# AdaLN half rows of a hybrid decoder layer: loads 0.6 of a spacing ahead, multiplies kept in program order, the loaded rows finished at a switch of buffers

## The chip, the cores and the metric

The kernel runs on one core of a Trainium2 chip. The metric is the device time of one execution in microseconds (us); lower is better. A profiled execution gives the trace from which the rows below are taken.

## The reference, cut to what matters

One decoder layer: a mixer of eight attention heads beside an RG-LRU recurrence, then an MLP. Each of the two halves of the layer is modulated by six vectors (shift, scale and gate for the mixer, the same for the MLP), which come from one product of the conditioning vector with a wide matrix.

```python
c_act = silu(c)                                     # [1, 2048]
mod = (c_act @ w_ada[l] + b_ada[l]).reshape(B, 6, 2048)
sh1, sc1, gt1, sh2, sc2, gt2 = mod

h = rmsnorm(x, g_norm_mix[l]) * (1.0 + sc1) + sh1
q, k, v, xr, xg = split(h @ w_in[l])                # 5 x 1024 columns, 512 tokens
o_attn = stick_breaking_attention(q, k, v)          # 8 heads of 128
xr = causal_depthwise_conv(xr, w_conv, b_conv)
o_lru = rg_lru(xr, ...) * gelu(xg)
mixed = concat(rmsnorm(o_attn), rmsnorm(o_lru))
x = x + gt1 * (mixed @ w_out[l])

h = rmsnorm(x, g_norm_mlp[l]) * (1.0 + sc2) + sh2
x = x + gt2 * (square(relu(h @ w_mlp_in[l])) @ w_mlp_out[l])
```

All of it is float32: 2048 model columns, 512 tokens, 8192 hidden columns.

## The kernel before

**Products.** TensorE (PE) does a float32 product as three products of fp32r operands: high weight by high operand, high weight by low operand, low weight by high operand (`mm3`, lines 259, 262 and 263; for v lines 467 to 469). `weights()` makes the two parts: SP, the engine that issues the loads, loads a raw block `wr`; ScalarE (ACT) copies it to `wh` (line 244, the high part); VectorE (DVE) subtracts that from `wr` to `wl` (line 122). There are four `wr` buffers and three each of `wh` and `wl`, and the three instructions are hoisted by a priority of 150. A step of a product is one such block: 12 matmuls over four PSUM banks. The banks are emptied by ACT (line 459, high part) and DVE (line 460, low part) for queries and keys.

**Attention and recurrence.** While the projections run, three lanes of background work (`bg`, `bgl`, `bg2`) are advanced by `tick()`, once for each step of a product. Each lane is a queue of generators that yield how many steps to wait. `bg` holds the pairs of attention heads: scores, their soft terms (ACT lines 637 to 639 and 644, DVE lines 635 and 641), `shares` (PE line 654) and values. `bgl` holds the recurrence: the convolution (DVE line 556), the gates (ACT line 566 and DVE line 122 split the input into an `x` tile, then PE; line 572 and 575 the sigmoids), and the scans (ACT lines 583, 587, 588 and 592, DVE lines 589, 595 and 597).

**AdaLN rows.** `bg2` holds `adas(m)` for the first gate GT1 and for the scale and shift of the MLP, SC2 and SH2. One of the 16 rows of such a vector is 128 of its columns, on 128 partitions: two half rows of the matrix, each 128 x 1024 (512 KB), loaded by SP (line 199), multiplied on DVE by the broadcast `silu(c)` in `cb` with a sum along the row (line 211), and joined by a small instruction (line 220). `pace` is the spacing of the rows in steps: 3.2 in the v product, 1.6 in the first eight steps of the product for heads 4 and 5, then 3.2 again.

**Buffers of the rows.** In the first part the half rows use the four `x` tiles alone (`MID`). These tiles hold also the split inputs of the gates and two tiles of each scan. Behind the product for the first half of the gate branch (`xg_group(0)`) the rows switch to `LATE`, which takes `x` and `tt` tiles in turn, with five half rows loaded ahead.

**Order.** A scheduler places the instructions of an engine by priority and by when their inputs are to be had, unless `later()` pins one: it then stays behind the instruction that was traced last before it on its engine. Loads of half rows are always pinned on SP. Their multiplies are pinned only in `LATE`, where each half is asked for by its number (`q` given). On the chip each engine does its instructions in the order so fixed.

Of the kernel before, what the change touches and what calls it, by code (L numbers as in the profile page):

```python
# [64 lines left out]
def hybrid_layer_kernel(  # L65
# [32 lines left out]
    def T(tag, dt=F32, cols=None):  # L98
        return new(next(split_tag) if tag == "w4" else tag, dt, cols)
# [48 lines left out]
    def col(base, j):  # L148
        return vec[:, base + j : base + j + 1]
# [29 lines left out]
    def later(ins):  # L179
        return tc.keep_in_program_order(ins)  # L180


    def mod(m, j):
        return mods[:, m * NK + j : m * NK + j + 1]

    class Rows:
# [15 lines left out]
        def row(self, m, j, tags, q=None):  # L202

            i = m * NK + j
            if q in (None, 0):
                self.ga = T("ga")
            for q_ in (0, 1) if q is None else (q,):
                if (i, q_) not in self.tiles:
                    self.load(2, tags)
                t = self.tiles.pop((i, q_))  # L210
                ins = stt(
                    out=t, in0=t, scalar=1.0, in1=cb[q_], op0=ALU.mult, op1=ALU.mult, accum_out=self.ga[:, q_ : q_ + 1],
                )
                if q is not None:
                    later(ins)
                del t
                if tags is not MID:
                    self.load(1, tags)
            if q != 0:
                stt(  # L220
                    out=mod(m, j), in0=self.ga[:, 0:1], scalar=self.ga[:, 1:2], in1=col(C_BADA, i), op0=ALU.add, op1=ALU.add,
                )

    rows, rows2 = Rows(SC1, SH1), Rows(GT1, SC2, SH2)
    MID = itertools.cycle(["x"])
# [73 lines left out]
    bg, bgl, bg2 = Lane(), Lane(), Lane()  # L299
# [300 lines left out]
    def lru_out(o0):  # L600
        for o in range(o0, o0 + 4):
            act(xg_t[o], xg_t[o], AF.Gelu_apprx_tanh)
        yield 1.0
        for o in range(o0, o0 + 4):
            g = xg_t[o]
            tt(out=g, in0=conv_y[o], in1=g, op=ALU.mult)
            add_square(acc_l, g, T("n"), o == 0)
            yield 1.0
# [89 lines left out]
    def adas(m):  # L698
        for j in range(NK):
            if tags2[0] is MID:  # L700
                rows2.row(m, j, MID)
                yield pace[0]
            else:
                for q in range(2):
                    rows2.row(m, j, LATE, q)
                    yield pace[0] / 2
        ready.add(m)

    pace = [3.2]
# [26 lines left out]
    def xg_group(o0, tags):  # L736
        bs = [bank(t) for t in tags]

        def evac(b):
            t = T("a")  # L740
            copy(b, t, bs[b])
            xg_t[o0 + b] = t

        group(bs, range(NK), lambda k: w_in[blk(k), XG + o0 * P : XG + (o0 + 4) * P], lambda k: hT[k], evac)
# [4 lines left out]
    bg.drain()  # L749
    bg.add(pair(2))  # L750
    bg2.add(adas(GT1), adas(SC2), adas(SH2))
    v_group(4)
    bg.drain()
# [14 lines left out]
    bg.add(attn_mix())  # L768
    bgl.add(lru_out(0))
    tags2[0] = LATE  # L770
    rows2.load(5, LATE)
    xg_group(4, BANKS[4:])
    bg.drain()
# [588 lines left out]
    tags = ["w4"] * 3 + ["w3"] * 2 + ["w4"] * 2 + ["w3"]  # L1362
# [108 lines left out]
```

## Time and profile before

| What | Value |
|---|---|
| Three timed runs | 1986.9, 1987.16, 1989.67 us; median 1987.16 |
| Profiled execution | 1982.96 us, of which the span is 1981.3 |
| Mean granted clock of TensorE | 0.996 |
| DVE line 211 from 237 to 530 us | 50 multiplies, 60.7 us, 1218 ns each |
| ACT table loads from 337 to 452 us | 13, 16.7 us |

A row of the timeline has the start and the duration in us, the engine, the line of the source, the operation, output and inputs, the shape of the tiles, and in brackets for how long the engine had been idle and what released it. A row of the groups has the count, then the busy time in us and the mean in ns, then the idle time ahead of it. A row of the waits has the engine, what it was about to write and its line, whom it waited for, the sum in us, how many times, and the longest. SPq is SP's own queue of instructions that issue loads; a row of the issues has the count, KB each, and the median time from issue to landing.

### The profile page before, as it was taken

To read this page: it belongs to the slowest core of one execution; us is meant where nothing else is said; L and a number is where in the kernel's file an instruction comes from. 1 tells how busy PE (TensorE), PEld (TensorE's weight loads), DVE (VectorE), ACT (ScalarE), POOL (GpSimd) and SP (SyncE) were. 2 spreads that over 40 slices of the span, in tenths; PEclk is the share of its full clock that TensorE was granted. 3 is DMA by queue.
4 is the path that set the end of the run, shared out by engine and by line. 5 is a ranking of instruction groups with operands and counts; after the bars stand their busy time and mean duration, and the time that the engine had idled before them with its cause. 6 is when DMAs were issued, how large, how long until landed. Compare 5 with 4: busy or idle time off the path is not lost.

```text
span 1981.3 us, 37180 instructions
## 1 busy us (share of the span) xinstructions
PE 1936.3 (98%) x14148; PEld 1813.5 (92%) x14148; DVE 1760.7 (89%) x2979; ACT 1077.1 (54%) x1580; POOL 193.4 (10%) x307
## 2 busy tenths in 40 slices
PE   8999999999999998999999999999999999999997
PEld 6778888788888998999999999999999999999996
DVE  8998786888998599999999999999989779879986
ACT  4443564786433386565555556556445545555542
POOL 0000000000000000112112211200000210211100
PEclk9999999999999999999999999999999999999998
DMA  9896655556779543756656665755677667669653
GB/s 365 306 331 214 205 172 186 183 157 217 226 244 373 176 139 114 239 187 223 211 182 196 223 194 184 235 186 195 234 260 284 247 249 269 232 248 343 215 198 112
DMA packets 205238, 443.51 MB, mean 224 GB/s; under 512 B 20481, under 2 KB 42113, under 8 KB 205058
## 3 DMA queue, kind: packets, MB, share of 16 engines
q1 hardware_dynamic: 176338, 356.58, 54.4%
q0 software_dynamic: 23680, 77.61, 10.6%
q10 hardware_dynamic: 5040, 6.93, 1.1%
q8 instruction: 111, 1.82, 0.4%
q14 instruction: 69, 0.57, 0.1%
HBM read 376.30 MB, written 64.75 MB: 223 GB/s over the span
## 4 chain that ended last, share of the span: by engine, by line
PE 53%; DVE 3%; DMA 1%; issue 1%; ACT 1%; POOL 0%; DVEq 0%; POOLq 0%; ACTq 0%; SPq 0%
PE ps_mm L1104 9%; PE ps_mm L1102 9%; PE ps_mm L1103 9%; PE ps_z L1103 7%; PE ps_z L1104 7%; PE ps_z L1102 7%; PE ps_o L1104 2%; PE ps_o L1102 2%; PE ps_o L1103 2%; DVE w L122 1%; DVE ts L1060 0%; DMA a<-sum 0%; DMA a<-part 0%; DVE a L1357 0%; DVE a L122 0%
## 5 line engine op out<-in xcount | busy, mean ns | idle before, releaser
L1102 PE MATMUL ps_mm<-a,w 128*128 128x256 f32 x1696 | 467.7, 276 | 1.5 <-ACT w L1072 0.5
L1103 PE MATMUL ps_mm<-a,w 128*128 128x256 f32 x1696 | 468.2, 276 | 0.3 <-DVE a L122 0.3
L1104 PE MATMUL ps_mm<-a,w 128*128 128x256 f32 x1696 | 468.1, 277 | 0.3 <-DVE w L122 0.3
L1104 PE MATMUL ps_z<-a,w 128*128 128x256 f32 x1304 | 361.1, 277 | 6.9 <-DVE w L122 6.7
L1103 PE MATMUL ps_z<-a,w 128*128 128x256 f32 x1304 | 360.7, 277 | 0.2
L1102 PE MATMUL ps_z<-a,w 128*128 128x256 f32 x1304 | 360.7, 277 | 0.1
L1072 ACT ACTIVATE w<-ts 128x1024 fp32r<-128x1024 f32 x244 | 258.2, 1058 | 169.6 <-DVE ts L1068 158.0
L1066 ACT ACTIVATE w<-raw 128x768 fp32r<-128x768 f32 x244 | 205.1, 841 | 259.5 <-PE ps_mm L1103 81.7
L122 DVE TENSOR_TENSOR w<-ts,w 128x1024 fp32r<-128x1024 f32 x244 | 297.7, 1220 | 52.9 <-PE ps_mm L1103 16.7
L1102 PEld LDWEIGHTS ps_mm<-a,w 128*128 128x128 f32 x1696 | 318.2, 188 | 2.1 <-ACT w L1072 0.7
L1104 PEld LDWEIGHTS ps_mm<-a,w 128*128 128x128 f32 x1696 | 318.4, 188 | 0.8 <-DVE w L122 0.7
L1103 PEld LDWEIGHTS ps_mm<-a,w 128*128 128x128 f32 x1696 | 318.5, 188 | 0.5 <-DVE a L122 0.5
L122 DVE TENSOR_TENSOR w<-raw,w 128x768 fp32r<-128x768 f32 (+1 forms) x296 | 267.2, 904 | 41.1 <-ACT w L244 24.9
L1104 PEld LDWEIGHTS ps_z<-a,w 128*128 128x128 f32 x1304 | 245.2, 188 | 8.2 <-DVE w L122 8.1
L1103 PEld LDWEIGHTS ps_z<-a,w 128*128 128x128 f32 x1304 | 245.3, 188 | 0.8 <-DVE a L122 0.8
L1102 PEld LDWEIGHTS ps_z<-a,w 128*128 128x128 f32 x1304 | 245.3, 188 | 0.5 <-ACT ps_z L1090 0.3
L244 ACT ACTIVATE wh<-wr 128x512 fp32r<-128x512 f32 (+1 forms) x184 | 113.2, 618 | 144.3 <-PE ps_mm L262 61.8
L259 PE MATMUL ps_mm<-a,wh 128*128 128x512 f32 x448 | 176.1, 393 | 2.4 <-ACT wh L244 1.2
L263 PE MATMUL ps_mm<-a,wl 128*128 128x512 f32 x448 | 174.8, 391 | 0.9 <-DVE wl L122 0.7
L262 PE MATMUL ps_mm<-a,wh 128*128 128x512 f32 x448 | 174.6, 390 | 0.0
L1060 DVE TENSOR_TENSOR ts<-raw 128x512 f32<-128x512 f32 x244 | 166.5, 683 | 6.4 <-DMA raw<-in_w_mlp_out_dram 5.6
L122 DVE TENSOR_TENSOR wl<-wr,wh 128x512 fp32r<-128x512 f32 (+1 forms) x184 | 123.5, 673 | 30.5 <-ACT wh L244 30.2
(334 smaller groups left out, 4011.2 us busy)
## 6 DMA issues: line engine op xcount, KB each, us to landing
raw<-in_w_mlp_out_dram SPq DMA_DIRECT2D x124, 512.0 KB, 4.6
raw<-in_w_mlp_in_dram SPq DMA_DIRECT2D x120, 512.0 KB, 3.8
x<-in_w_adaT_dram SPq DMA_DIRECT2D x108, 512.0 KB, 5.4
wr<-in_w_in_dram SPq DMA_DIRECT2D x160, 256.0 KB, 3.3
tt<-in_w_adaT_dram SPq DMA_DIRECT2D x52, 512.0 KB, 6.4
part<-a POOLq DMA_DIRECT2D x84, 256.0 KB, 4.2
a<-part SPq DMA_DIRECT2D x84, 256.0 KB, 6.2
n<-in_w_adaT_dram SPq DMA_DIRECT2D x64, 256.0 KB, 4.2
```

What stands on the lines that cost most here:

```text
L122: tt(out=out, in0=full, in1=f32(high), op=ALU.subtract)
L244: act(h[:, :n], r[:, :n], AF.Copy)
L259: first = mm(out, wh, ah, start=start, stop=False, **kw)
L262: mm(out, wh, al, start=False, stop=False, **kw)
L263: mm(out, wl, ah, start=False, stop=stop, **kw)
L1060: tt(out=t[:, : 2 * HT].rearrange("p (a b) -> p a b", a=2), in0=r[:, HT : 3 * HT].rearrange("p (a b) -> p a b", a=2), in1=r[:, q_(0)].unsq ...
L1066: act(h, r[:, HT:], AF.Copy)
L1072: act(h, t, AF.Copy)
L1102: mm(out, wh[:, blk(i)], ah, start=st, stop=False, **kw)
L1103: mm(out, wh[:, blk(i)], al, start=False, stop=False, **kw)
L1104: mm(out, wl[:, blk(i)], ah, start=False, stop=j == js[-1], **kw)
```

## The change

```diff
@@ class Rows, row()
                 ins = stt(
                     out=t, in0=t, scalar=1.0, in1=cb[q_], op0=ALU.mult, op1=ALU.mult, accum_out=self.ga[:, q_ : q_ + 1],
                 )
-                if q is not None:
+                if q is not None or tags is MID:
                     later(ins)
@@ def adas(m)
             if tags2[0] is MID:
+                rows2.load(2, MID)
+                yield 0.6 * pace[0]
                 rows2.row(m, j, MID)
-                yield pace[0]
+                yield 0.4 * pace[0]
@@ behind xg_group(0)
     tags2[0] = LATE
+    while rows2.tiles:
+        bg2.next()
     rows2.load(5, LATE)
     xg_group(4, BANKS[4:])
```

In `MID` a row's two loads are issued 0.6 of the spacing before its multiplies; the multiplies are pinned behind the DVE instruction traced last; and at the switch to `LATE` the rows that have been loaded are multiplied before the five loads ahead are issued. The number of loads, multiplies and matmuls is the same. The lines of the changed kernel stand two or four further down behind the added ones. The order of all engines moves with it from the v product on to the second half of the gate branch, in three places as follows. In the rows a name is a tile with its running number, `x` a half row or a tile of the recurrence, `ga` the two sums of a row, `wr`, `wh` and `wl` a block of weights and its parts, `ps_` a PSUM bank, `a` and `n` work tiles, `vec` and `spl` constants.

DVE near the end of the v product, where the last v banks are emptied (line 484) and the product for heads 4 and 5 begins, before:

```order
L484 TENSOR_TENSOR a_2857<-ps_mm_2389,a_2856 128x256
L211 SCALAR_TENSOR_TENSOR x_3000,ga_2999<-x_3000,cb_81 128x1024
L484 TENSOR_TENSOR a_2861<-ps_mm_2389,a_2860 128x256
L484 TENSOR_TENSOR a_2857<-ps_mm_2390,a_2856 128x256
L211 SCALAR_TENSOR_TENSOR x_3002,ga_2999<-x_3002,cb_82 128x1024
L484 TENSOR_TENSOR a_2861<-ps_mm_2390,a_2860 128x256
L220 SCALAR_TENSOR_TENSOR mods<-ga_2999,vec 128x1
L362 TENSOR_TENSOR n_1849<-n_1849,tt_2768 128x512
L484 TENSOR_TENSOR a_2898<-ps_mm_2391,a_2897 128x256
L211 SCALAR_TENSOR_TENSOR x_3026,ga_3025<-x_3026,cb_81 128x1024
L122 TENSOR_TENSOR wl_2948<-wr_2945,wh_2947 128x512
```

DVE at the same place in the changed kernel:

```order
L484 TENSOR_TENSOR a_2853<-ps_mm_2389,a_2852 128x256
L484 TENSOR_TENSOR a_2857<-ps_mm_2389,a_2856 128x256
L484 TENSOR_TENSOR a_2853<-ps_mm_2390,a_2852 128x256
L484 TENSOR_TENSOR a_2857<-ps_mm_2390,a_2856 128x256
L362 TENSOR_TENSOR n_1849<-n_1849,tt_2764 128x512
L484 TENSOR_TENSOR a_2898<-ps_mm_2391,a_2897 128x256
L211 SCALAR_TENSOR_TENSOR x_2812,ga_2887<-x_2812,cb_81 128x1024
L122 TENSOR_TENSOR wl_2944<-wr_2941,wh_2943 128x512
```

Of three multiplies ahead of the block of weights one is left.

DVE between the masks of the first scores of heads 4 and 5 and the first line 641 of that head, which the shares wait for through ACT, before:

```order
L597 SCALAR_TENSOR_TENSOR a_2386<-a_1028,a_2386 128x512
L122 TENSOR_TENSOR wl_3526<-wr_3523,wh_3525 128x512
L595 TENSOR_TENSOR a_2473<-x_3282,a_2473 128x512
L595 TENSOR_TENSOR a_2516<-x_3282,a_2516 128x512
L597 SCALAR_TENSOR_TENSOR a_2473<-a_1030,a_2473 128x512
L597 SCALAR_TENSOR_TENSOR a_2516<-a_1032,a_2516 128x512
L556 SCALAR_TENSOR_TENSOR a_3511<-a_1034,vec,a_3511 128x511
L211 SCALAR_TENSOR_TENSOR x_3516,ga_3515<-x_3516,cb_81 128x1024
L122 TENSOR_TENSOR wl_3575<-wr_3572,wh_3574 128x512
L122 TENSOR_TENSOR wl_3629<-wr_3626,wh_3628 128x512
L556 SCALAR_TENSOR_TENSOR a_3511<-a_1034,vec,a_3511 128x510
L641 SCALAR_TENSOR_TENSOR tt_3433<-ps_z_3418,tt_3433 128x512
```

DVE at the same place in the changed kernel:

```order
L597 SCALAR_TENSOR_TENSOR a_2386<-a_1028,a_2386 128x512
L595 TENSOR_TENSOR a_2469<-x_3282,a_2469 128x512
L122 TENSOR_TENSOR wl_3571<-wr_3568,wh_3570 128x512
L597 SCALAR_TENSOR_TENSOR a_2469<-a_1030,a_2469 128x512
L595 TENSOR_TENSOR a_2516<-x_3282,a_2516 128x512
L211 SCALAR_TENSOR_TENSOR x_3388,ga_3468<-x_3388,cb_81 128x1024
L211 SCALAR_TENSOR_TENSOR x_3390,ga_3468<-x_3390,cb_82 128x1024
L122 TENSOR_TENSOR wl_3629<-wr_3626,wh_3628 128x512
L641 SCALAR_TENSOR_TENSOR tt_3429<-ps_z_3414,tt_3429 128x512
```

A scan (line 597) and two steps of the convolution (line 556) have moved behind line 641, and the two multiplies of a row stand side by side ahead of it.

ACT in the first recurrence, where its functions change between the sigmoids of the gates (lines 572 and 575) and the functions of the scans (lines 583 and 587), before:

```order
L575 ACTIVATE ps_z_3135<-ps_z_3135,vec 128x512
L583 ACTIVATE x_3281<-a_1026,spl 128x512
L1422 ACT_TABLE_LOAD
L244 ACTIVATE wh_3210<-wr_3208 128x256
L587 ACTIVATE a_1026<-a_1026,nspl 128x512
L1422 ACT_TABLE_LOAD
L244 ACTIVATE wh_3227<-wr_3225 128x512
L572 ACTIVATE a_1028<-ps_z_3168,vec 128x512
```

ACT at the same place in the changed kernel:

```order
L575 ACTIVATE ps_z_3215<-ps_z_3215,vec 128x512
L583 ACTIVATE x_3281<-a_1026,spl 128x512
L244 ACTIVATE wh_3297<-wr_3295 128x512
L583 ACTIVATE x_3281<-a_1028,spl 128x512
L244 ACTIVATE wh_3323<-wr_3321 128x512
L572 ACTIVATE a_1032<-ps_z_3248,vec 128x512
L575 ACTIVATE ps_z_3253<-ps_z_3253,vec 128x512
L583 ACTIVATE x_3282<-a_1030,spl 128x512
L583 ACTIVATE x_3282<-a_1032,spl 128x512
L1426 ACT_TABLE_LOAD
L244 ACTIVATE wh_3329<-wr_3327 128x512
L587 ACTIVATE a_1026<-a_1026,nspl 128x512
```

The four instructions of line 583 now stand together ahead of the first of line 587, and the table is loaded once between them.

## The prediction

> **What bounds the kernel now.** I read the page's share of the engines first, then the windows of the stretch that the change touches (from the output projection on, past 530 us, every engine's order is the old one), then the waits of PE and of DVE in that stretch.
>
> ```profile
> PE 1936.3 (98%) x14148; PEld 1813.5 (92%) x14148; DVE 1760.7 (89%) x2979; ACT 1077.1 (54%) x1580; POOL 193.4 (10%) x307
> ...
> core 0: us, PE busy (x) PEld busy (x) DVE busy (x) ACT busy (x) POOL busy (x), PEclk, DMA share, GB/s
> 237.00:300.00 63.00, 63.00 (x316) 53.76 (x315) 49.02 (x84) 41.11 (x61) 0.00 (x0) 1.00 0.49 160
> 300.00:350.00 50.00, 49.23 (x218) 40.10 (x218) 31.63 (x62) 25.01 (x45) 0.00 (x0) 1.00 0.60 192
> 350.00:400.00 50.00, 47.50 (x222) 38.67 (x222) 46.65 (x80) 38.00 (x58) 0.00 (x0) 1.00 0.57 179
> 400.00:452.00 52.00, 50.63 (x240) 41.50 (x239) 42.28 (x73) 47.48 (x72) 0.00 (x0) 1.00 0.57 174
> 452.00:520.00 68.00, 68.00 (x319) 57.19 (x319) 58.88 (x96) 38.81 (x60) 3.51 (x1) 1.00 0.66 214
> ```
>
> PE is busy 98% of the span. In the first and the last of these windows it is never idle, in the three between it lacks 0.77 + 2.50 + 1.37 = 4.64 us of 152. DVE is nearly full only from 350 to 400, ACT only from 400 to 452. So a change that moves DVE work can win only what PE waits here, and the next view names it:
>
> ```profile
> engine line waited for: us in total, times, longest us
> PE ps_z L654 <- ACT tt L644: 1.8, 2, 1.4
> PE ps_z L654 <- DVE tt L122: 1.0, 2, 0.8
> PE ps_mm L259 <- DVE a L460: 0.8, 1, 0.8
> PE ps_mm L263 <- DVE wl L122: 0.7, 1, 0.7
> ...
> DVE x L211 <- DMA x<-in_w_adaT_dram: 15.4, 10, 3.6
> SPq L199 <- DVE x L211: 23.5, 12, 5.6
> ```
>
> These are all of PE's waits from 237 to 530 us: 1.8 + 1.0 + 0.8 + 0.7 = 4.3 us, 0.22% of the run. The wait that the change aims at, DVE's for the half rows, is far larger, 15.4 us in 10 pieces, but it is idle time of an engine that PE waited for only in those four rows. The last row is SP's own: an x load stands at the head of its queue until a tile is free, up to 5.6 us, and weight loads stand behind it.
>
> **The change part by part.** The number of multiplies and of loads stays. What moves:
>
> ```profile
> L211 DVE SCALAR_TENSOR_TENSOR x<-x,cb 128x1024 f32<-128x1024 f32 x50 | 60.7, 1218 | 15.6 <-DMA x<-in_w_adaT_dram 15.4
> x<-in_w_adaT_dram SPq DMA_DIRECT2D x52, 512.0 KB, 4.7
> wr<-in_w_in_dram SPq DMA_DIRECT2D x78, 256.0 KB, 2.8
> ```
>
> A multiply costs 1.22 us, a row's pair 2.44; a half row lands 4.7 us after its issue (median). The early load buys 0.6 of the spacing: at pace 3.2 that is 1.92 weight steps, at pace 1.6 (the first eight steps of the products for heads 4 and 5) 0.96. A step is one weight load of 256 KB, 78 of them in these 293 us, so about 3.8 us with the attention beside it (an estimate: 293/78). The lead is then near 7.2 us, over the 4.7, and near 3.6, under it. I expect most of the 15.4 us to go and a few to stay. The pin costs no instruction; what it does is to fix behind which DVE instruction each pair stands. Five places come out of the new order.
>
> *First: the end of the v product.*
>
> ```profile
> 307.22 1.23 DVE L211 SCALAR_TENSOR_TENSOR x<-x,cb 128x1024 f32<-128x1024 f32 x1 [1.36 <-DMA x<-in_w_adaT_dram]
> 309.04 1.21 DVE L211 SCALAR_TENSOR_TENSOR x<-x,cb 128x1024 f32<-128x1024 f32 x1
> 311.66 1.21 DVE L211 SCALAR_TENSOR_TENSOR x<-x,cb 128x1024 f32<-128x1024 f32 x1
> 312.81 1.29 DVE L122 TENSOR_TENSOR wl<-wr,wh 128x512 fp32r<-128x512 f32 x2
> 313.54 0.50 PE L263 MATMUL ps_mm<-a,wl 128*128 128x512 f32 x1 [0.72 <-DVE wl L122]
> ```
>
> Three multiplies and a landing stand just ahead of the weights' low part for which PE waits 0.72 us. In the new order one stands there, so 2 x 1.22 + 1.36 = 3.8 us of DVE leave that place, five times the wait: **-0.7**. What is late next is the high part on ACT, half busy there (25.01 of 50).
>
> *Second: the fourth bank of the product for heads 4 and 5.*
>
> ```profile
> 364.11 1.22 DVE L211 SCALAR_TENSOR_TENSOR x<-x,cb 128x1024 f32<-128x1024 f32 x1
> 365.25 0.69 DVE L122 TENSOR_TENSOR wl<-wr,wh 128x512 fp32r<-128x512 f32 x1
> 365.86 0.68 DVE L460 SCALAR_TENSOR_TENSOR a<-ps_mm,a 128x512 fp32r<-128x512 f32 x1
> 363.71 0.59 ACT L459 ACTIVATE a<-ps_mm 128x512 fp32r<-128x512 f32 x1
> 366.59 0.50 PE L259 MATMUL ps_mm<-a,wh 128*128 128x512 f32 x1 [0.77 <-DVE a L460]
> ```
>
> The bank's high part was ready at 363.71 + 0.59 = 364.30, yet L460 began at 365.86, behind a multiply and a weight. In the new order no multiply stands between the third and the fourth L460. The 1.22 us exceed PE's 0.77: **-0.8**.
>
> *Third: the first shares of heads 4 and 5.*
>
> ```profile
> 376.61 0.73 DVE L556 SCALAR_TENSOR_TENSOR a<-a,vec,a 128x511 f32<-128x511 f32 x1
> 379.61 0.74 DVE L556 SCALAR_TENSOR_TENSOR a<-a,vec,a 128x510 f32<-128x510 f32 x1
> 374.36 2.33 DVE L597 TENSOR_TENSOR_SCAN a<-a,a 128x512 f32<-128x512 f32 x2
> 380.26 1.61 DVE L641 SCALAR_TENSOR_TENSOR tt<-ps_z,tt 128x512 f32<-128x512 f32 x3
> 381.97 1.27 ACT L644 ACTIVATE tt<-tt 128x1280 fp32r<-128x1280 f32 x1 [2.97 <-DVE tt L641]
> 383.29 0.50 PE L654 MATMUL ps_z<-tt,ntri 128*128 128x512 f32 x1 [1.37 <-ACT tt L644]
> ```
>
> PE waits 1.37 us for ACT, which waited 2.97 for DVE's three L641. Between the third L460 and L641, DVE had three multiplies and has four now (+1.22), but one scan (2.33/2 = 1.17) and two steps of the convolution (0.73 + 0.74) move behind L641: 1.42 us less. PE reaches the shares three matmuls later in its order (an estimate from the first window: 3 x 63.00/316 = 0.6), but the 0.77 of the second place sooner. So the slack grows by 1.42 + 0.6 - 0.77 = 1.25; of the 1.37 I take **-1.1**, with 0 and -1.4 as ends.
>
> *Fourth: the first shares of heads 6 and 7.*
>
> ```profile
> 446.39 1.27 ACT L644 ACTIVATE tt<-tt 128x1280 fp32r<-128x1280 f32 x1 [0.71 <-DVE tt L641]
> 450.10 0.50 PE L654 MATMUL ps_z<-tt,ntri 128*128 128x512 f32 x1 [0.77 <-DVE tt L122]
> L244 ACT ACTIVATE wh<-wr 128x512 fp32r<-128x512 f32 (+1 forms) x184 | 113.2, 618 | 144.3 <-PE ps_mm L262 61.8
> L583 ACT ACTIVATE x<-a,spl 128x512 f32<-128x512 f32 x8 | 5.5, 720 | 0.0
> ```
>
> Here ACT decides. Two L583, one L587 (about the same length) and one high part stand ahead of L644 now that stood behind it: 3 x 0.72 + 0.62 = 2.78 us, less ACT's own 0.71 of waiting and the 0.6 that PE comes later, but with 1.28 less for each table load that has left the stretch ahead (below), of which I count one: +0.2, ends -0.5 and +1.5. The second half of the shares waited 0.77 for its low part (L122, behind the multiply of 446.21) and has one matmul more in between and no multiply: I count -0.5. Together **-0.3**.
>
> *Fifth: the gates of the last recurrence.* The low part of gate 6 now stands behind a multiply pair, about 8 us later than before, and PE's order puts eleven other matmuls ahead of the gate's last one. The windows give PE 240 matmuls in 52 us, so these cover 2.4 us, the pair takes 2.44: **0**, with 0 and +2.4 as ends.
>
> *The tables of ACT.* The new order has four table loads fewer, two in each recurrence:
>
> ```profile
> L1422 ACT ACT_TABLE_LOAD x13 | 16.7, 1283 | 0.2
> 415.54 1.28 ACT L1422 ACT_TABLE_LOAD   x1
> 416.83 0.42 ACT L244 ACTIVATE wh<-wr 128x256 fp32r<-128x256 f32 x1
> ```
>
> 4 x 1.283 = 5.1 us leave ACT. PE names ACT only in the 1.8 us of the two shares, which the third and fourth place hold already, so I add 0 beyond them. The Trainium skill, page "ScalarE: Activation LUTs", section "What ACT_TABLE_LOAD costs", puts a switch at 1283 ns plus a drain of about 1380 ns, 2.66 us: four would be 10.6 us of ACT by that page, an estimate. The trace agrees on the load, 1283 ns; of a drain it shows nothing here, since the next instruction begins 1.29 us after the load's start (415.54 to 416.83).
>
> *The finish before the switch to LATE.* The rows already loaded are multiplied at once there, and two rows more fall into 452 to 520. PE is full there without a gap and DVE has 68 - 58.88 = 9.1 us free; two rows are 4 x 1.22 = 4.9: 0. Without that room it would be up to +4.9.
>
> **The sum**: -0.7 - 0.8 - 1.1 - 0.3 + 0 = -2.9 us. The profiled execution took 1982.96 us (span 1981.3), 4.2 us under the median of the three timed runs, 1987.16, and below all of them; against itself the sum gives 1980.1, on the median 1984.3. The ends: -0.7 - 0.8 - 1.4 - 1.3 = -4.2, and -1.5 + 0 + 1.5 + 2.4 = +2.4.
>
> **Rivals.** *All waits go.* If nothing new comes late, PE wins the 4.3 us, and with the 4.64 of the windows as the largest sum that they show, 1982.9 to 1982.5. That the four rows are PE's only named waits speaks for it; the longer ACT queue ahead of the fourth and the pinned pairs against it.
>
> *ACT is the path from 400 to 452.* ACT is busy 47.48 of 52 us there, and if PE's gaps follow ACT's lag in both recurrences, the four table loads come off in full: 5.1 us, 1982.0. Against it: PE lacks only 1.37 us in that window, so at least 3.7 of it could come only from matmuls that overlap more closely. The page above would make it 10.6; the row's 1.283 bounds it.
>
> *The change misses its mark.* Loads are in SP's order behind weight loads and behind full tiles (23.5 us of such waits); at pace 1.6 the lead of 3.6 us is under the 4.7 of landing. Then the pinned multiplies wait as before, and only the second place gains: -0.8, 1986.4. The 2.97 us that ACT waits at the third place would stay.
>
> *Slower: a pinned pair holds DVE where PE is next.* DVE works in order, so a pair that stands ahead of gate 6's low part, of L641 at the third place, or of the fourth place's chain holds PE for its own length. It decides where PE's cover is under 2.44 us, and at the fifth place 2.4 stand against 2.44. Three such places are 3 x 2.44 = 7.3 us, less the 1.5 of the first two: +5.8, 1993.0. For it: DVE is 46.65 of 50 busy in the window of the third place. Against it: multiplies stood unpinned at the first two places and cost PE no more than 0.7 and 0.8 us there.
>
> **How the numbers follow.** About 0.2%, 4.0 us, is what a measurement of this kernel can tell from no change: faster means below 1983.2, slower above 1991.1. My forecast, -2.9 with its own range 1982.8 to 1986, has 0.47, of which 0.07 lies below 1983.2. All waits go: 0.17, faster. ACT as the path: 0.10, faster. The mark missed: 0.15, same. The held pairs: 0.11, slower. That is 0.34 faster, 0.55 same, 0.11 slower. The range reaches from 1980.5, below the second rival, to 1989.5, the +2.4 of the terms; beyond it lies most of the last case and a little below.
>
> **What would show it.** In the changed kernel's profile DVE's wait of 15.4 us for the half rows should fall to under 5; PE's waits for wl at L263 and for L460 should be gone; those for L644 should be at most 1 us in sum; table loads in 337 to 452 should be 9 in place of 13. A row of PE waiting at the gate's L262 or L263 for DVE would show the fifth term wrong, and a PE wait for wh on ACT near 400 to 452 that has gone would speak for ACT as the path. I am wrong if PE's idle time from 300 to 452 grows, or shrinks by over 4 us.

## The result, and the profile after

The changed kernel takes 1982.32 us (median of 22 runs, 1978.1 to 1984.99) against 1984.35 us for the kernel before (22 runs, 1981.03 to 1989.67). The ratio is 0.9983 with a 95% interval of 0.9977 to 0.9989, so 2.2 to 4.6 us less, while the two medians lie only 2.0 us apart; a second set of runs (below) gives 0.9990, 0.9979 to 1.0000, with 1.5 us between its medians. The forecast was 2.9 us less. The profiled execution of the changed kernel took 1984.99 us, the slowest of its 22, so totals of two profiles say nothing here; their parts do.

The page of the changed kernel, then its windows of the changed stretch (columns as before):

```profile
PE 1936.9 (98%) x14148; PEld 1814.7 (92%) x14148; DVE 1760.3 (89%) x2979; ACT 1071.8 (54%) x1576; POOL 193.2 (10%) x307
```

```profile
300.00:350.00 50.00, 50.00 (x224) 41.14 (x223) 35.01 (x68) 22.86 (x43) 0.00 (x0) 1.00 0.69 217
350.00:400.00 50.00, 46.66 (x222) 38.64 (x220) 44.74 (x77) 37.68 (x57) 0.00 (x0) 1.00 0.55 177
400.00:452.00 52.00, 51.22 (x243) 42.03 (x242) 41.36 (x71) 45.91 (x73) 0.00 (x0) 1.00 0.44 140
```

PE has gained 0.77 us from 300 to 350 and 0.59 from 400 to 452, and has lost 0.84 between them. The waits of the changed kernel from 237 to 530 us, of PE, DVE and SP's queue:

```profile
PE ps_z L654 <- ACT tt L644: 1.5, 1, 1.5
PE ps_mm L259 <- DVE a L460: 1.2, 1, 1.2
PE ps_z L654 <- DVE tt L122: 0.9, 2, 0.6
PE ps_z L259 <- ACT tt L663: 0.2, 1, 0.2
...
DVE x L211 <- DMA x<-in_w_adaT_dram: 1.4, 2, 0.9
...
SPq L199 <- DVE x L211: 46.1, 29, 6.5
```

DVE's wait for the half rows fell from 15.4 to 1.4 us, by 14.0. PE's named waits fell from 4.3 to 3.8 us. So 14 us of idle time went from an engine that PE seldom waits for. SP's loads wait for free tiles twice as long as before (46.1 against 23.5 us), and none of PE's rows names a load.

How long did PE need for the stretch itself? These are its first matmul of the second v product and the matmul that waits for the first weights of the output projection, in the timelines of the kernel before and of the changed one:

```profile
253.88 0.39 PE L467 MATMUL ps_mm<-wh,a 128*128 128x512 f32 x1
548.15 0.50 PE L259 MATMUL ps_mm<-a,wh 128*128 128x512 f32 x1 [0.46 <-ACT wh L244]
```

```profile
253.48 0.39 PE L467 MATMUL ps_mm<-wh,a 128*128 128x512 f32 x1
547.02 0.50 PE L259 MATMUL ps_mm<-a,wh 128*128 128x512 f32 x1 [0.77 <-ACT wh L244]
```

That is 294.27 us before and 293.54 after, 0.73 less. Below, "the stretch" is this difference of two starts. The matmul at its end waits itself, for the high part `wh`, and longer after the change (0.77 against 0.46).

### The profile page after: what moved, and what is told of

Its sections match the earlier page's. It is cut to its first block, busy times and chain, and to the rows that moved or that the text cites. A ratio compares the mean times of both kernels' runs of the same rounds, so it can differ in the third digit from the quotient of the medians.

```text
span 1983.2 us, 37201 instructions
## 1 busy us (share of the span) xinstructions
PE 1936.9 (98%) x14148; PEld 1814.7 (92%) x14148; DVE 1760.3 (89%) x2979; ACT 1071.8 (54%) x1576; POOL 193.2 (10%) x307
## 4 chain that ended last, share of the span: by engine, by line
PE 50%; DVE 6%; DMA 2%; issue 1%; ACT 1%; POOL 0%; DVEq 0%; SPq 0%; POOLq 0%; ACTq 0%
PE ps_mm L1108 8%; PE ps_mm L1106 8%; PE ps_mm L1107 8%; PE ps_z L1107 6%; PE ps_z L1108 6%; PE ps_z L1106 6%; PE ps_o L1108 2%; PE ps_o L1106 2%; PE ps_o L1107 2%; DVE w L122 2%; DMA raw<-in_w_mlp_out_dram 1%; DVE ts L1064 1%; DVE a L1361 1%; DVE a L122 0%; DMA a<-part 0%
## 5 line engine op out<-in xcount | busy, mean ns | idle before, releaser
L122 DVE TENSOR_TENSOR w<-ts,w 128x1024 fp32r<-128x1024 f32 x244 | 297.9, 1221 | 53.0 <-PE ps_mm L1108 17.0
L122 DVE TENSOR_TENSOR w<-raw,w 128x768 fp32r<-128x768 f32 (+1 forms) x296 | 267.7, 905 | 41.9 <-ACT w L244 25.6
L263 PE MATMUL ps_mm<-a,wl 128*128 128x512 f32 x448 | 174.6, 391 | 0.1
L122 DVE TENSOR_TENSOR wl<-wr,wh 128x512 fp32r<-128x512 f32 (+1 forms) x184 | 123.4, 674 | 33.8 <-ACT wh L244 30.8
```

The costliest lines, as they stand in the source:

```text
L122: tt(out=out, in0=full, in1=f32(high), op=ALU.subtract)
L263: mm(out, wl, ah, start=False, stop=stop, **kw)
```

## The experiments

The theory that stands behind the forecast: what counts is **where** the multiplies stand in DVE's order, at the few places where PE is next (called "order" in the expectations). Rivals: DVE's wait for the half rows is itself worth the time ("landing"); the four table loads fewer are ("tables"); or the gain is not in this stretch at all ("spread").

**Both kernels again.** No edit; a second profile and more runs of each.

> The kernel before, a second profile. Theory 'order' (the gain is what PE no longer waits between the v product and the second half of the gate branch): PE needs again about 294.3 us from its first v matmul (L467) to its wait for wh near 548 us, within 0.3, and the waits of 0.7 (L263 for wl), 0.8 (L259 for L460) and 1.4 us (L654 for ACT) are there again. Rival 'spread' (these waits differ from execution to execution, and the gain lies elsewhere): that stretch differs by over 0.7 us from the first profile. The timed ratio should be 1.000 within 0.001.

> The changed kernel, a second profile. Theory 'order': the same stretch takes 293.5 us within 0.3 as in its first profile, the wait for wl at L263 is gone, those of 1.2 (L259 for L460) and 1.5 us (L654 for ACT) stand; then the stretch gives only 0.7 of the 3.4 us measured. Rival 'spread': the stretch is 2 us or more shorter than in before2. Ratio 0.998.

Measured: 1.0005 (0.9994 to 1.0016) for the kernel before against itself, 0.9990 for the changed one. The stretch took 295.10 us before and 294.16 after. So it repeats within 0.8, not 0.3, and the differences in favour of the changed kernel, 0.73 and 0.94 in the two pairs, are of that size. Its waits repeat within a hundredth at the second and third place (1.25 and 1.45 us). The first place does not repeat: in the second profile of the kernel before that row reads

```profile
PE ps_mm L263 <- DVE wl L122: 1.3, 1, 1.3
```

and in neither profile of the changed kernel is there a wait at this place. "Spread" is half true: the kernel before differs from itself by over 0.7 us, as it says, but the changed kernel is not 2 us ahead in the stretch, as it also says. The stretch accounts for 0.7 to 0.9 us, the timed runs say 2 to 3.4.

**The pin alone, and the early loads alone.**

```diff
 e_pin: the kernel before, with
-                if q is not None:
+                if q is not None or tags is MID:
 e_load: the kernel before, with
+                rows2.load(2, MID)
+                yield 0.6 * pace[0]
                 rows2.row(m, j, MID)
-                yield pace[0]
+                yield 0.4 * pace[0]
...
+    while rows2.tiles:
+        bg2.next()
```

> Pin alone, loads still issued right before their multiplies. Theory 'order': the pinned multiplies wait for their loads on DVE (4.7 us each to land, the 15.4 us of before grow to 30 or more) and hold weights behind them; ratio 1.000 to 1.004. Rival 'tables' (the gain comes from ACT's table loads, 18 here against 20 before and 16 in the changed kernel): half the gain, ratio 0.999. Rival 'landing' (the gain is DVE's wait for half rows): no gain or a loss.

> Early loads and the finish before LATE, multiplies not pinned. Table loads 20 as before. Theory 'order': the multiplies float as before, so PE's waits at L263 and L460 stay in part; DVE's waits for the half rows fall from 15.4 to under 4; ratio 0.999 to 1.000. Rival 'landing': the full gain, 0.998. Rival 'tables': none, 1.000.

Measured: 1.0004 (0.9995 to 1.0013) for the pin, 1.0022 (1.0013 to 1.0031) for the early loads, which is 4.4 us slower than before. Neither part has the gain. For the early loads I had expected 0.999 to 1.000, and on what the parts do to DVE I was wrong twice. The waits with the pin alone, PE's and DVE's:

```profile
PE ps_z L654 <- ACT tt L644: 1.4, 2, 1.2
PE ps_mm L259 <- ACT wh L244: 1.3, 1, 1.3
PE ps_mm L263 <- DVE wl L122: 1.0, 1, 1.0
PE ps_z L259 <- ACT tt L663: 1.0, 1, 1.0
...
DVE x L211 <- DMA x<-in_w_adaT_dram: 5.3, 3, 2.7
```

The pin cuts DVE's wait to 5.3 us, though the program issues no load sooner; I had expected 30 or more. PE's waits do not go, they move: none near 313, but 1.0 for the gate at 407 us, 1.3 for wh at 422 and 1.0 for a wl at 380. With the early loads alone DVE's wait doubles to 30.2 us, where I had expected under 4, and PE waits 3.4 us at the first place:

```profile
307.74 1.23 DVE L211 SCALAR_TENSOR_TENSOR x<-x,cb 128x1024 f32<-128x1024 f32 x1 [3.73 <-DMA x<-in_w_adaT_dram]
...
315.37 1.23 DVE L211 SCALAR_TENSOR_TENSOR x<-x,cb 128x1024 f32<-128x1024 f32 x1 [3.10 <-DMA x<-in_w_adaT_dram]
317.45 0.69 DVE L122 TENSOR_TENSOR wl<-wr,wh 128x512 fp32r<-128x512 f32 x1
```

The second of these held DVE 3.10 us and pushed the wl of 317.45, for which PE waited. So in this run the unpinned multiplies were still put ahead of their data although the loads were issued sooner; only with the pin did the lead become real. The pin alone takes 10 us of DVE's wait away and gains nothing, so "landing" is not what the total goes by.

**The table load at the second place.** The profile of the changed kernel, ACT, then DVE, then PE, at the fourth bank of the product for heads 4 and 5:

```profile
358.71 0.60 ACT L459 ACTIVATE a<-ps_mm 128x512 fp32r<-128x512 f32 x1
...
360.46 1.28 ACT L1426 ACT_TABLE_LOAD   x1
361.75 0.63 ACT L244 ACTIVATE wh<-wr 128x512 fp32r<-128x512 f32 x1
362.29 0.58 ACT L459 ACTIVATE a<-ps_mm 128x512 fp32r<-128x512 f32 x1
```

```profile
362.42 0.69 DVE L122 TENSOR_TENSOR wl<-wr,wh 128x512 fp32r<-128x512 f32 x1 [1.60 <-ACT wh L244]
363.03 0.68 DVE L460 SCALAR_TENSOR_TENSOR a<-ps_mm,a 128x512 fp32r<-128x512 f32 x1
```

```profile
363.76 0.50 PE L259 MATMUL ps_mm<-a,wh 128*128 128x512 f32 x1 [1.24 <-DVE a L460]
```

No multiply stands there, as forecast, but DVE idles 1.60 us: ACT's table load now lies between the third bank and the fourth (358.71 and 362.29). In the kernel before it lay between the first and the second, where PE had no wait:

```profile
357.64 0.58 ACT L459 ACTIVATE a<-ps_mm 128x512 fp32r<-128x512 f32 x1
359.36 1.28 ACT L1422 ACT_TABLE_LOAD   x1
360.66 0.60 ACT L459 ACTIVATE a<-ps_mm 128x512 fp32r<-128x512 f32 x1
```

The next run takes it away by leaving the square roots out:

```diff
-            act(m[i], m[i], AF.Sqrt)
+            act(m[i], m[i], AF.Square)
```

> The changed kernel with the square roots of the recurrence (line 592 of before) replaced by squares, which leaves the square root out; six of its 16 table loads go with it, one of them the load ahead of the fourth bank's high part (L459). Theory 'table': that load, 1.28 us on ACT, is what now holds the fourth bank, so PE's wait for L460 falls from 1.2 us to under 0.3, and its wait of 1.5 us for ACT at the shares, which follow on the same ACT and DVE rows, to under 1.0. Rival 'DVE': the weights and L589 on DVE hold it, and both waits stay within 0.3. Time against before 0.997 to 0.999.

Measured: 0.9974 (0.9965 to 0.9984), and PE's waits are these two rows alone:

```profile
PE ps_z L654 <- ACT tt L644: 1.2, 2, 0.9
PE ps_z L654 <- DVE tt L122: 0.5, 2, 0.3
```

The wait for L460 is gone and the one at the first shares is 0.9 in place of 1.5. Between the third and the fourth bank DVE has the same instructions here as in the changed kernel (two low parts of weights, L122), so the table load is the cause of the first wait. The 0.6 us of the second can't be put down to it: in this run three multiplies stand between the fourth bank and line 641 in place of four. The stretch took 290.44 us.

**The same without leaving anything out.** The square root as exp(0.5 ln(.)), in the changed kernel and in the kernel before:

```diff
-            act(m[i], m[i], AF.Sqrt)
+            act(m[i], m[i], AF.Ln); act(m[i], m[i], AF.Exp, scale=0.5)
```

> The changed kernel with the square root of the recurrence worked out as exp(0.5 ln(.)) on ACT: the same mathematics, 8 more activations of 0.62 us, table loads 10 in place of 16, none of them between the third and the fourth bank of the product for heads 4 and 5. Theory 'table': PE's wait of 1.2 us for L460 goes as in the run with the square root left out; ratio 0.9965 to 0.9985, with the four more activations late for the scans (under 0.6 us at the shares). Rival 'DVE': wait stays, 0.998 to 1.000.

> The kernel before, with the square root as exp(0.5 ln(.)) too; table loads 14 in place of 20. Theory 'order' (the change's own gain is that multiplies leave the places where PE waits): the waits of 0.7 to 1.3 us (wl at L263) and 0.8 us (L460) behind multiplies stay here and are absent in the changed kernel with the same square root; ratio 0.999 to 1.000, 0.1 to 0.25% above that kernel. Rival 'tables' (the change gains only through its four table loads fewer): as fast as that kernel within 0.05%.

Measured: 0.9983 (0.9974 to 0.9992) on the changed kernel, median 1980.75 us, and 1.0002 (0.9993 to 1.0011) on the kernel before, 1984.64. PE's waits, changed kernel first:

```profile
PE ps_z L654 <- ACT tt L644: 1.9, 2, 1.4
PE ps_z L654 <- DVE tt L122: 0.8, 2, 0.6
```

```profile
PE ps_z L654 <- ACT tt L644: 2.5, 2, 1.8
PE ps_mm L263 <- DVE wl L122: 1.2, 1, 1.2
PE ps_z L654 <- DVE tt L122: 0.8, 2, 0.5
```

The wait for L460 went in both. In the kernel before I had expected it to stay behind a multiply; it did not, since the order moved with the square root and no multiply stands between its third and fourth L460 any more. So that run does not tell the multiply from the table load at this place. The wait for wl at L263 stayed there, as expected. In the changed kernel the wait at the first shares stays at 1.41 us with no table load between the banks and the shares. With the same square root the change is worth 0.19%, about as much as with the old one, and six table loads fewer (14 against 20) gave the kernel before nothing. That nothing holds a loss: the mean granted clock of its timed runs is 0.9951, that of the kernel before beside it 0.9957, which is about 1.2 us (an estimate: 0.0006 of 1984). Counted out, about 0.1% between the two kernels remains, so the number of table loads alone is not what the change gains by. Against the changed kernel itself, whose two ratios are 0.9983 and 0.9990, this version is not measurably faster, though its stretch is the shortest of all that compute everything (291.50 us).

**How much the multiplies cost at all.** Each cut to 64 of its 1024 columns, which leaves 15/16 of these sums out:

```diff
+                u = slice(0, 64) if tags is MID else slice(0, 1024)
                 ins = stt(
-                    out=t, in0=t, scalar=1.0, in1=cb[q_], ...
+                    out=t[:, u], in0=t[:, u], scalar=1.0, in1=cb[q_][:, u], ...
```

> The changed kernel with each multiply of the MID half rows cut to 64 of 1024 columns, which leaves 15/16 of those sums out: some 46 us of DVE go, the loads stay, table loads 18. Theory 'order': DVE's multiplies hold PE at single places only, the most that can be won is the 3.8 us of named waits, and the part of them that ACT causes stays: 0 to 2.5 us under the changed kernel, ratio 0.997 to 0.9985. Rival 'DVE load': 4 us or more under the changed kernel, ratio under 0.9965.

Measured: 0.9988 (0.9977 to 0.9998), no faster than the changed kernel. PE still waits for ACT at the shares, longer than before:

```profile
PE ps_z L655 <- ACT tt L645: 3.1, 2, 2.2
```

I had expected 0.997 to 0.9985. What holds DVE at the shares here is no multiply: three steps of the convolution have moved ahead of its line 641 (642 in this run):

```profile
377.11 2.06 DVE L557 SCALAR_TENSOR_TENSOR a<-a,vec,a 128x511 f32<-128x511 f32 x3
```

So with nearly all of the multiplies' DVE time gone there is no further gain in this order, and "DVE load" falls. That their amount is worth nothing in any order is not shown: the order of the other engines moved with the cut too (11 table loads from 337 to 455 us against 9), and the mean granted clock of these runs is 0.9948, against 0.9956 for the kernel before beside them.

**Other leads, phases and no finish.**

```diff
 e_lead9: the changed kernel, with
-                yield 0.6 * pace[0]
+                yield 0.9 * pace[0]
...
-                yield 0.4 * pace[0]
+                yield 0.1 * pace[0]
 e_nodrain: the changed kernel, without
-    while rows2.tiles:
-        bg2.next()
 e_phase4 (and e_phase8 with 0.8): the changed kernel, with
-    bg2.add(adas(GT1), adas(SC2), adas(SH2))
+    bg2.add(iter([0.4]), adas(GT1), adas(SC2), adas(SH2))
```

> The changed kernel with the loads 0.9 of a spacing ahead in place of 0.6; table loads 14. Theory 'order': DVE's wait for the half rows (1.4 to 2.4 us) goes to under 1, worth nothing to PE; the fourth bank still has a table load ahead of it, so PE waits there again; ratio 0.998 to 0.9995. Rival 'landing' or 'tables': a further 0.1%, ratio 0.9975 or less.

> The changed kernel without the finish of the loaded rows at the switch to LATE: the loaded row is then multiplied in two steps after the switch. Theory 'order': nothing of it is on PE's path, 0.998 to 0.9995, with the waits of 1.2 and 1.5 us as in the changed kernel. Rival: the finish is what frees the window from 452 to 520 us, then 1.000.

> The changed kernel with the rows begun 0.4 of a step later, nothing else; 16 table loads, the one of the first recurrence now behind the fourth bank's high part instead of ahead of it, and two multiply pairs between the fourth L460 and L641 as before. Theory 'table' and 'order': PE's wait of 1.2 us for L460 is under 0.4, that at the shares within 0.5 of 1.5; ratio 0.997 to 0.9985. Rival: the wait stays at 1.2.

> The changed kernel with the rows begun 0.8 of a step later; 16 table loads, one of them ahead of the fourth bank's high part as in the changed kernel. Theory 'order': the places of the pairs and not the early loads decide, so PE's wait for L460 is 0.9 to 1.4 again, and the sum of PE's named waits from 237 to 530 us differs from the changed kernel's 3.8 by up to 2 either way; ratio 0.998 to 1.0005. Rival 'landing': the loads are as early, so the same 0.998 to 0.9985.

| Run | Ratio (95%) | The stretch, us | PE's named waits 237 to 530, us | DVE waits for half rows, us |
|---|---|---|---|---|
| changed, both profiles | 0.9983 and 0.9990 | 293.54, 294.16 | 3.8, 4.5 | 1.4, 2.4 |
| e_lead9 | 1.0000 (0.9990 to 1.0010) | 295.71 | 5.3 | 7.1 |
| e_nodrain | 0.9985 (0.9974 to 0.9996) | 294.90 | 5.3 | 2.6 |
| e_phase4 | 1.0013 (1.0001 to 1.0026) | 295.85 | 4.7 | 9.0 |
| e_phase8 | 1.0003 (0.9994 to 1.0012) | 296.81 | 5.5 | 6.6 |

A start 0.4 or 0.8 of a step later, with the same lead, takes the whole gain away, so the gain hangs on the places that 0.6 and this start happen to give, not on loading ahead as such. Part of that loss is the clock of TensorE: the mean granted clock of the timed runs is 0.9940 in e_phase4 and 0.9948 in e_phase8 and e_lead9, against 0.9956 to 0.9961 in the kernel before, the changed kernel and e_nodrain. At 2.0 us for each thousandth of 1984 us (an estimate) that is 1.5 to 3.3 us, as much as the gain itself; the last section has the rows. In e_phase4 the table load lies behind the fourth bank and PE has no wait for L460, as "table" says; but the wait at the shares grew to 2.2 us where I had expected 1.0 to 2.0, and my ratio (under 0.9985) was wrong. In e_phase8 the table load is ahead of the fourth bank again, and the wait is 1.24 us, as "order" says. In e_lead9 I expected DVE's wait under 1 us and it was 7.1, and a ratio of 0.998 to 0.9995: a longer lead did not shorten the wait, and the gain was gone. The finish is free in the total, but not idle: without it PE waits 1.4 us for a wl at 479 us, in the changed kernel 0 and 0.6.

## Why the prediction was right, and where its steps failed

The total was right: 2.9 us forecast, 2.2 to 4.6 measured (2.0 by the medians). Its terms were not: of the five places only the first came out as forecast, and all together they gave 0.4 us. So the total is right by luck as far as these terms go: most of the gain comes from nothing in the sum. As an absolute time it was too high: 1984.3 was worked out from the first three runs' median of 1987.16, which is 2.8 us above the median of all 22, and the measured 1982.32 lies 0.5 us below the forecast's own range of 1982.8 to 1986, though inside the whole one. The other rows on which this rests, of the changed kernel, PE and then DVE and ACT:

```profile
382.18 0.50 PE L654 MATMUL ps_z<-tt,ntri 128*128 128x512 f32 x1 [1.46 <-ACT tt L644]
...
384.72 0.50 PE L654 MATMUL ps_z<-tt,ntri 128*128 128x512 f32 x1 [0.65 <-DVE tt L122]
...
405.84 0.49 PE L259 MATMUL ps_z<-x,wh 128*128 128x512 f32 x1 [0.25 <-ACT tt L663]
...
446.89 0.50 PE L654 MATMUL ps_z<-tt,ntri 128*128 128x512 f32 x1
...
449.08 0.50 PE L654 MATMUL ps_z<-tt,ntri 128*128 128x512 f32 x1 [0.30 <-DVE tt L122]
```

```profile
370.81 0.69 DVE L122 TENSOR_TENSOR wl<-wr,wh 128x512 fp32r<-128x512 f32 x1 [0.78 <-ACT wh L244]
...
377.40 1.22 DVE L211 SCALAR_TENSOR_TENSOR x<-x,cb 128x1024 f32<-128x1024 f32 x1
...
379.15 1.61 DVE L641 SCALAR_TENSOR_TENSOR tt<-ps_z,tt 128x512 f32<-128x512 f32 x3
...
380.85 1.27 ACT L644 ACTIVATE tt<-tt 128x1280 fp32r<-128x1280 f32 x1 [3.32 <-DVE tt L641]
```

| Place | Forecast | Named wait before, two profiles | After, two profiles | Change |
|---|---|---|---|---|
| First (wl at the end of the v product) | -0.7 | 0.72, 1.32 | 0, 0 | -0.7, -1.3 |
| Second (fourth bank) | -0.8 | 0.77, 0.75 | 1.24, 1.25 | +0.5, +0.5 |
| Third (first shares of heads 4, 5) | -1.1 | 1.56, 1.54 | 2.11, 2.11 | +0.6, +0.6 |
| Fourth (first shares of heads 6, 7) | -0.3 | 1.23, 1.27 | 0.30, 0.32 | -0.9, -1.0 |
| Fifth (gates of the last recurrence) | 0 | 0, 0 | 0.25, 0.24 | +0.2, +0.2 |
| The finish | 0 | 0, 0 | 0, 0.61 | 0, +0.6 |

(The third and the fourth are sums over both halves of the shares.) The changes add up to -0.4 us in each pair. The wait at the end of the stretch, past the 530 us at which the prediction stopped, takes 0.3 back (0.46 and 0.47 before, 0.77 and 0.81 after).

- **First: right.** The multiplies left, the wait is gone in both profiles. The pin does it: with the pin alone it is gone too, with the early loads alone it is 3.4 us.
- **Second: wrong, in sign.** The step "the 1.22 us exceed PE's 0.77" looked at DVE alone. I had the new order of ACT before me and costed its table loads by their number, four fewer, for nothing; I did not look where the remaining ones stand. One moved between the third and the fourth bank. Two runs without it, and one with it behind the fourth bank, have no such wait; three others with it there (e_nodrain, e_phase8, e_lead9) wait 1.24, 1.24 and 0.76 us.
- **Third: wrong.** I counted DVE's instructions and put its waits at nothing. Its work from the third L460 to L641 did shrink, by about 1.0 us (1.42 forecast), but DVE now idles 1.60 + 0.78 us and a third time 0.29 in between, waiting for ACT's wh, where it did not idle before: 19.0 us in place of 17.4. The slack of 1.25 us that I counted was used up there. How much of the wait is the table load's is open (0.90 us are left without square roots, 1.41 with exp and ln, both without the load). So is what the multiply pair costs that ends one weight ahead of L641 (377.40): in the run with the multiplies cut, other work moved into their place.
- **Fourth: right in sign, too small.** I had ACT late by 0.2; the first half's wait of 0.46 went. The ACT instructions that I had counted ahead of L644 did not hold PE. The second half fell from 0.77 to 0.30, the -0.5 that I had counted, but not because a multiply left: one still stands right ahead of its low part, at 446.39.
- **Fifth:** gate 6 caused no wait. The first gate of that recurrence did, for the bank that ACT's L663 frees, with 0.25 us. Right behind it (406.43) a weight load of PE waits 0.4 us for the low part of that gate's input, which stands on DVE behind a pinned pair (402.27) and a step of the convolution: what I feared for gate 6, at a gate that I had not looked at, and in a row of PEld, not of PE.
- **The cap.** That DVE's 15.4 us are no measure of the gain held: 14.0 of them went. The slower rival didn't come about in the changed kernel, but its mechanism is real: held on DVE for 3.10 us, PE lost 3.4 in e_load. "The change misses its mark" was wrong: the loads land in time. "All waits go" was wrong too: 3.8 of the 4.3 us stayed. "ACT is the path" is not borne out: PE won 0.59 us from 400 to 452, not 5.1.
- **The signs.** DVE's wait under 5 us, no wait for wl at L263 near 313 and 9 table loads came true; no wait for L460 (1.2) and at most 1 us for L644 (1.5) did not.

What stays open is size. PE's named waits give 0.4 us, and 0.1 or less with the wait at the end of the stretch; the stretch gives 0.7 to 0.9 of the 2 to 3.4 that the timed runs show. That much is seen in the waits of the weight loads (PEld), which also show breaks too short for PE's own rows. Over the whole stretch they add up to 10.4 us before and 9.7 after, 11.5 and 10.2 in the second pair, and the row of the weights' low part alone falls by 1.3 and 1.5; in the first pair, before and then after, it reads:

```profile
PEld ps_mm L263 <- DVE wl L122: 2.0, 3, 1.1
```

```profile
PEld ps_mm L263 <- DVE wl L122: 0.7, 2, 0.5
```

For the stretch that agrees with the theory. What lies behind the stretch has the same order on every engine in both kernels, and it took 1429.9 to 1438.7 us in the fourteen profiles, which is more than the gain; in the changed kernel's two it was longer (1436.2 and 1434.5) than in the two of the kernel before (1433.2 and 1429.9). I have not found the rest of the gain.

## What to carry to other kernels

Read a wait by who waits for the waiter: 14 us of DVE's idle time went for a gain of 2 to 3.4, and with the pin alone 10 us went for none. When a change reorders engines, follow each place through every engine on its chain, ACT's table loads too: their position, not only their number. A gain that goes when the same code starts 0.4 of a step later is a fit of places; in these runs loading ahead paid only together with pinning the consumers. At differences of 0.1%, compare the granted clock of the runs before reading their times.

## What the runs showed of the hardware that was not expected

A wait of PE can cost more than its length. In e_phase4 PE waited 2.19 us at the shares; windows ahead of it and behind, the granted clock is the column after POOL:

```profile
370.00:381.00 11.00, 11.00 (x50) 9.13 (x49) 10.08 (x19) 8.43 (x12) 0.00 (x0) 1.00 0.68 220
383.00:390.50 7.50, 6.43 (x25) 5.81 (x26) 7.32 (x11) 3.69 (x6) 0.00 (x0) 0.61 0.56 187
390.50:400.00 9.50, 9.50 (x45) 8.06 (x44) 8.21 (x15) 5.62 (x9) 0.00 (x0) 0.95 0.32 107
```

and matmuls of 128x512 that followed each other every 0.23 us ahead of the wait take 0.42 behind it:

```profile
380.59 0.39 PE L259 MATMUL ps_mm<-a,wh 128*128 128x512 f32 x1
380.82 0.39 PE L262 MATMUL ps_mm<-a,wh 128*128 128x512 f32 x1
...
389.19 0.63 PE L262 MATMUL ps_z<-a,a 128*128 128x512 f32 x1
389.61 0.63 PE L263 MATMUL ps_z<-a,a 128*128 128x512 f32 x1
```

The 0.61 is a mean over 7.50 us, so the clock cost about 2.9 us there (an estimate: 0.39 of 7.50). The clock fell behind the long waits of five other runs too. As means over 5.5 to 6.6 us it was 0.74 behind 1.80 us in the kernel before with the new square root, behind 1.89 in e_lead9, behind 2.16 in e_small and behind 1.35 in e_phase8, and 0.69 behind 3.43 in e_load. It stayed at 1.00 behind the 1.37 us of the kernel before, the 1.46 of the changed one and a wait of 1.70 in e_load. So from 1.35 to 1.70 us length alone does not decide it. The timed runs show the same: their mean granted clock is 0.9940 to 0.9951 in these six kernels and 0.9955 to 0.9961 in all others. The Trainium skill, page "TensorE: Matmul & The Clock Gate", section "What's actually happening", tells of a gate that falls back after an idle window of about 3.4 us, with windows that run free of the kernel. That the outcome differs at like lengths agrees with free-running windows, but here waits well under 3.4 us were enough.
